# A two-layer decoder trunk in float32: which operand of its large products stands still

## Chip, core and metric

One core of one Trainium2 chip runs the whole program. The metric is the time of one execution in device microseconds (us), as the median of several runs.

## The reference

The reference takes 256 tokens of 2048 features through two layers, all in float32, and returns 256 x 2048 numbers. Cut to what matters:

```python
# layer 0
h = rms_norm(x) * (1 + scale0) + shift0          # scale, shift, gate = silu(c) @ ada_w + ada_b
p = h @ hg_w_in[0]                               # 2048 x 7440
x = x + gate0 * (concat(rwkv7(p), gated_deltanet(p)) @ hg_w_out[0])     # 2048 x 2048
x = x + gate1 * swiglu(rms_norm(x) * (1 + scale1) + shift1)             # 2 x 2048 x 5632, 5632 x 2048
# layer 1
p = modulated_norm(x) @ ssm_w_in[0]              # 2048 x 10304
x = x + gate2 * (mamba2(p) @ ssm_w_out[0])       # 4096 x 2048
x = x + gate3 * swiglu(modulated_norm(x))
return rms_norm(x) * final_norm_w
```

`swiglu(h)` is `(silu(h @ w1) * (h @ w3)) @ w2`. The mixers (RWKV-7, gated DeltaNet, Mamba-2) are recurrences over the tokens, worked in chunks of 128 tokens. The four modulations are products of one row, `silu(c)`, with four matrices of 2048 x 6144.

## The kernel before

**Large products.** Everything is kept with features on the partitions: an activation is 16 row blocks (kt) of 128 features x 256 tokens. A weight matrix is cut into tiles of 128 x 128. A product is made in float32 accuracy from two narrow parts of each operand: `split` (line 743) writes the rounded `hhi` and the rest `hlo`; `split_next` (line 623) rounds the weights to `whi` on the scalar engine (ACT) and `low_parts` (line 657) takes the rest `wlo` on the vector engine (DVE). `products` (line 703) then issues three matmuls for each weight tile: the weight tile is the stationary operand, the 256 tokens move through it.

```python
PE.matmul(ps, w(hi, i), ahi[:, kt, :], start=a, stop=False)
PE.matmul(ps, w(hi, i), alo[:, kt, :], start=False, stop=False)
...
PE.matmul(ps, w(lo, i - lag), ahi[:, kt, :], start=False, stop=z)
```

The sum, 128 features x 256 tokens, takes half a bank of PSUM. `lin_tile` (line 678) makes one such column block over all kt. `lin_slab` (line 729) opens a phase: it takes 7 or 8 column blocks at once, kt by kt, so that it can begin when the norm has made the first row block; `clear` (line 725) first writes zeros into each of its banks, with one matmul of 512 columns.

**Streams.** All weights come in the order of their use, up to 1024 columns x 128 rows (512 KB) at a time, through SyncE's queue (SP) into five raw tiles. The modulation weights come in between as half rows; each is a multiply and reduce on DVE (`ada_half`, line 584), 384 in all.

**Phases.** Layer 0's input projection (`in0`, 59 column blocks, with zeros that fill up one of them), the mixers beside it, the output projection (`out0`, begun while the last heads still run), a SwiGLU (`ffn`, line 824, in two halves of the hidden features), layer 1's input projection (`in1`, 81 column blocks, half of one filled up with zeros) beside the Mamba mixer, its output projection (`out1`, two halves), a second SwiGLU. The results of `out0`, `ffn` and `out1` go tile by tile into `out_tiles` (line 803): DVE adds gate times the sum to `x`, ACT squares, DVE sums the squares for the next norm.

**Order.** The program has one order per engine, made while it is traced. A model of the engines' times (`Clock`, line 233) says when each instruction runs. The mixers are chains of small steps (`spawn`, line 458); `products` looks at them after each weight tile, and `run` (line 444) places a step once the model has it ready 600 ns before TensorE's (PE's) present place. `force` (line 464) places steps, soonest first, until a condition holds, whether or not the engines have to wait for them; `bank` (line 413) calls it where fewer than four banks are free for a new sum. So PE, DVE and ACT run in a fixed order in which the chains' instructions stand between those of the stream.

**What takes a sum from PSUM.** With features on the partitions, the convolution (`conv_silu`, line 1024), the token shift (`shift`, line 1227), the gates (`z_gate`, line 1245, and `gate_part`, line 1678), the SwiGLU product (in `ffn`) and `out_tiles` read the sums directly. Only two narrow blocks are turned to tokens on partitions, by `tok_major` (line 1055).

## Time and profile before

| | |
|---|---|
| median of 3 runs | 3018.11 us (3016.45 to 3021.1) |
| the profiled execution: first to last instruction | 3020.2 us |
| TensorE (PE) busy | 2876.4 us, 95% |
| its weight loads (PEld) busy | 2804.5 us, 93% |
| DVE busy | 2216.3 us, 73% |
| ACT busy | 1436.8 us, 48% |
| read from HBM | 695.70 MB |

A row of the timeline gives start, length, engine and operation of one instruction, or of several alike in succession (x4); a matmul names the bank that it writes, then its moving and its stationary operand. PE's matmuls are pipelined: each is listed with its whole length, though the next starts long before it ends, so the price of one in a stream is the distance from its start to the next one's. A row of the stages gives for a stretch of time the busy time and instruction count of each engine, the clock granted to PE, the DMA share and GB/s. Nearly all instructions carry one source line, L351, that of a helper that records them.

### The profile page before, as it was taken

To read this page: it belongs to the slowest core of one execution; us is meant where nothing else is said; L and a number is where in the kernel's file an instruction comes from. 1 tells how busy PE (TensorE), PEld (TensorE's weight loads), DVE (VectorE), ACT (ScalarE), POOL (GpSimd) and SP (SyncE) were. 2 spreads that over 40 slices of the span, in tenths; PEclk is the share of its full clock that TensorE was granted. 3 is DMA by queue.
4 is the path that set the end of the run, shared out by engine and by line. 5 is a ranking of instruction groups with operands and counts; after the bars stand their busy time and mean duration, and the time that the engine had idled before them with its cause. 6 is when DMAs were issued, how large, how long until landed. Compare 5 with 4: busy or idle time off the path is not lost.

```text
span 3020.2 us, 61379 instructions
## 1 busy us (share of the span) xinstructions
PE 2876.4 (95%) x25033; PEld 2804.5 (93%) x25033; DVE 2216.3 (73%) x3546; ACT 1436.8 (48%) x2353; POOL 115.0 (4%) x159
## 2 busy tenths in 40 slices
PE   3699999998799999999999999999999999999998
PEld 3599898988799999999999999999999999999998
DVE  6988888988677787777767878888867754554555
ACT  2254555545444444444446556555445444444444
POOL 0000001000000000000000111111000000000000
PEclk8799999999999999999999999999999999999999
DMA  7977566667687898877865666666866756656554
GB/s 278 355 250 222 175 201 215 188 223 287 220 283 275 280 334 312 286 269 262 262 207 203 204 215 228 215 232 218 283 223 221 278 189 176 199 184 192 185 173 153
DMA packets 236667, 706.29 MB, mean 234 GB/s; under 512 B 37296, under 2 KB 56032, under 8 KB 236128
## 3 DMA queue, kind: packets, MB, share of 16 engines
q1 hardware_dynamic: 235808, 699.46, 68.9%
q8 instruction: 195, 3.19, 0.4%
q10 hardware_dynamic: 576, 2.92, 0.3%
q14 instruction: 88, 0.72, 0.1%
HBM read 695.70 MB, written 6.58 MB: 233 GB/s over the span
## 4 chain that ended last, share of the span: by engine, by line
issue 51%; PE 21%; DVE 2%; ACT 1%; POOL 0%; DMA 0%; DVEq 0%; POOLq 0%; ACTq 0%
PE bank L351 21%; DVE wlo L351 1%; ACT whi L351 1%; DVE hlo L351 0%; DVE adat L351 0%; DVE t0b L351 0%; DVE x L351 0%; DVE w L351 0%; POOL mgsa L351 0%; DVE ymix L351 0%; DMA adat<-in_ada 0%; DVE mar L351 0%; ACT t L351 0%; DVE mxs L351 0%; ACT hhi L351 0%
## 5 line engine op out<-in xcount | busy, mean ns | idle before, releaser
L351 PE MATMUL bank<-hhi,whi 128*128 128x256 f32 x5568 | 1485.8, 288 | 71.0 <-ACT whi L351 68.8
L351 PE MATMUL bank<-hlo,whi 128*128 128x256 f32 x5568 | 1459.6, 284 | 2.9 <-DVE hlo L351 2.6
L351 DVE TENSOR_TENSOR wlo<-raw,whi 128x1024 fp32r<-128x1024 f32 (+3 forms) x997 | 1111.0, 1128 | 393.8 <-ACT whi L351 389.9
L351 ACT ACTIVATE whi<-raw 128x1024 fp32r<-128x1024 f32 (+3 forms) x997 | 965.2, 977 | 697.5 <-PE bank L351 641.6
L351 PEld LDWEIGHTS bank<-hhi,whi 128*128 128x128 f32 x5568 | 1066.1, 191 | 95.7 <-ACT whi L351 79.3
L351 PE MATMUL bank<-hhi,wlo 128*128 128x256 f32 x5568 | 1131.3, 285 | 6.3 <-DVE wlo L351 5.9
L351 PEld LDWEIGHTS bank<-hlo,whi 128*128 128x128 f32 x5568 | 1067.2, 192 | 6.6 <-DVE hlo L351 4.6
L351 PEld LDWEIGHTS bank<-hhi,wlo 128*128 128x128 f32 x5568 | 864.8, 191 | 15.0 <-DVE wlo L351 9.2
L351 PE MATMUL bank<-ghi,whi 128*128 128x256 f32 x1408 | 351.2, 282 | 0.2 <-ACT whi L351 0.2
L351 PE MATMUL bank<-glo,whi 128*128 128x256 f32 x1408 | 351.2, 282 | 0.0
L351 PEld LDWEIGHTS bank<-ghi,whi 128*128 128x128 f32 x1408 | 265.1, 188 | 0.4 <-ACT whi L351 0.4
L351 PEld LDWEIGHTS bank<-glo,whi 128*128 128x128 f32 x1408 | 265.2, 188 | 0.0
L351 PE MATMUL bank<-ghi,wlo 128*128 128x256 f32 x1408 | 229.7, 282 | 0.0
L351 DVE CUSTOM_DVE_ANT_0 adat<-adat,silc,adap 128x1024 f32<-128x1024 f32 x160 | 211.8, 1323 | 21.4 <-DMA adat<-in_ada 20.6
L351 DVE CUSTOM_DVE_ANT_0 adat<-adat,silc,prm 128x1024 f32<-128x1024 f32 x160 | 208.4, 1303 | 14.2 <-DMA adat<-in_ada 14.1
L351 PEld LDWEIGHTS bank<-ghi,wlo 128*128 128x128 f32 x1408 | 193.9, 188 | 0.0
L351 ACT ACTIVATE fs<-bank 128x256 f32<-128x256 f32 x88 | 33.7, 383 | 189.2 <-PE bank L351 189.2
L351 DVE TENSOR_TENSOR fg<-fs,bank 128x256 f32<-128x256 f32 x88 | 37.0, 421 | 115.2 <-ACT fs L351 115.2
L351 DVE SCALAR_TENSOR_TENSOR w<-pad,prm,w 128x256 f32<-128x256 f32 x216 | 110.1, 511 | 5.1
L351 DVE SCALAR_TENSOR_TENSOR x<-bank,mod,x 128x256 f32<-128x256 f32 x106 | 50.6, 482 | 45.9 <-PE bank L351 45.5
L351 POOL TENSOR_TENSOR rstd<-rpow,half_neg 128x2 f32<-128x2 f32 x5 | 4.4, 890 | 1768.6 <-DVE rpow L351 1768.6
L351 DVE TENSOR_TENSOR glo<-fg,ghi 128x256 fp32r<-128x256 f32 x88 | 37.4, 425 | 42.6 <-ACT ghi L351 42.6
(251 smaller groups left out, 2011.5 us busy)
## 6 DMA issues: line engine op xcount, KB each, us to landing
raw<-in_ffn SPq DMA_DIRECT2D x352, 512.0 KB, 4.4
adat<-in_ada SPq DMA_DIRECT2D x320, 512.0 KB, 4.5
raw<-in_in SPq DMA_DIRECT2D x266, 512.0 KB, 3.8
raw<-in_ffn SPq DMA_DIRECT2D x128, 384.0 KB, 4.5
raw<-in_ffn SPq DMA_DIRECT2D x128, 320.0 KB, 3.0
raw<-in_out SPq DMA_DIRECT2D x75, 512.0 KB, 4.6
raw<-in_ada SPq DMA_DIRECT2D x64, 512.0 KB, 5.3
mar<-sscr SPq DMA_DIRECT2D x16, 512.0 KB, 7.7
```

Source lines behind the costliest of these rows:

```text
L351: r = f(*a, **k)
```

## The change

The large products swap their operands. The stationary operand is now a 128 features x 128 tokens block of the activation, and up to 512 columns of weights move through it. Each row block of weights and column block of width w takes six matmuls: for both halves of the tokens the high and the low part of the activation against `hi`, then the high part against `lo`. The sum has tokens on the partitions and fills two banks (`pair`), one for each half of the tokens. Column blocks are 512 wide in both `ffn`, in `out1`, in the z gates and in half of `out0`; 384 wide (three heads' columns; once 400 and once 448, with the narrow blocks that were filled up with zeros before) in the rest of the projections; 256 wide twice. A piece of weights still holds at most 1024 columns: two units of 384 or 512.

What reads the sums still wants features on the partitions. So a sum is copied from PSUM to SBUF (`evac`, or the first step of a gate or of SwiGLU, or the addition of an earlier part), and `turn` brings each 128 columns of it back with two transposes on TensorE, two blocks into one bank; then the old steps follow. The SwiGLU product is taken with tokens on partitions and turned once. The first half of `ffn` is kept in SBUF with tokens on the partitions, instead of being added to `x`. `clear`, `tok_major` and the zeros are gone. The order of layer 0's heads is another, and the order model has new prices for the stream's matmuls. Comments are dropped too. The core of the diff:

```diff
-ORDER0 = [(q[0], int(q[1:])) for q in "r0 r1 g0 r2 z0 r3 g1 r4 z1 r5 g2 r6 r7 g3 z2 z3".split()]
+ORDER0 = [(q[0], int(q[1:])) for q in "r0 r1 r2 g0 r3 z0 g1 r4 r5 g2 r6 r7 g3 z1".split()]
...
+LAG = 3
...
+def _in0():
+    out, c = [(0, 256)], 256
+    for k, j in ORDER0:
+        for n in {"r": [400 if j == 2 else 384], "g": [384, 384], "z": [512]}[k]:
+            out.append((c, n))
+            c += n
+    return out
+def _in1():
+    out, c = [], 0
+    for g in range(8):
+        for n in (448 if g == 0 else 384, 384, 512):
+            out.append((c, n))
+            c += n
+    return out
+IN0, IN1 = _in0(), _in1()
+SLAB0, SLAB1 = 3, 2
...
+def by_cols(block, kts=range(16), m=0):
+    c, n = block
+    kts, w = list(kts), COLS // n
+    return [[(m, k, c, n) for k in kts[i:i + w]] for i in range(0, len(kts), w)]
...
-    def release(t):
-        busy.discard(next(q for q in range(8) if banks[q] is t))
+    def pair(spare=SPARE):
+        force(lambda: len(busy) <= 6 - spare)
+        return [bank(True, 0) for _ in range(2)]
+    def release(*ts):
+        for t in ts:
+            busy.discard(next(q for q in range(8) if banks[q] is t))
...
-    def lin_tile(ps, act, kts, first=True, last=True):
...
+    def lin(acc, block, act, kts=range(KT), first=True, last=True, need=None):
...
+            products([(acc, k, n, first and k == a, last and k == z) for _, k, _, n in us], hi, lo, act)
+            del kts[:len(us)]
...
+    def slab(accs, act, ahead):
+        for kt in range(KT):
+            for k in range(LEAD + 1 if kt == 0 else 1):
+                k = kt + LEAD if kt else k
+                if k < KT:
+                    ahead(k)
+            hi, lo, us = next_piece()
+            assert [u[1] for u in us] == [kt] * len(accs)
+            products([(acc, kt, u[3], kt == 0, kt == KT - 1) for acc, u in zip(accs, us)], hi, lo, act)
...
+    def products(us, hi, lo, act):
+        n = len(us)
         lag = min(LAG, n)
+        at = [sum(u[2] for u in us[:i]) for i in range(n)]
+        def tick():
+            low_parts()
+            issue_raw()
+            run()
+            if max(clock.at(ET.DVE), clock.at(ET.Activation)) < clock.at(ET.PE) + SOON:
+                prefetch()
+            fill_ada()
         for i in range(n + lag):
             if i < n:
+                acc, k, w, a, z = us[i]
+                for t in range(2):
+                    for e in range(2):
+                        PE.matmul(acc[t][:, :w], act[:, k, e, t * P:(t + 1) * P], hi[:, at[i]:at[i] + w],
+                                  start=a and e == 0, stop=False)
+                    tick()
             if i >= lag:
+                acc, k, w, a, z = us[i - lag]
+                for t in range(2):
+                    PE.matmul(acc[t][:, :w], act[:, k, 0, t * P:(t + 1) * P],
+                              lo[:, at[i - lag]:at[i - lag] + w], start=False, stop=z)
+                tick()
...
-    def clear(b):
-        PE.matmul(b, zeros.to_broadcast([P, P]), zeros.to_broadcast([P, 512]), start=True, stop=False)
...
+    def evac(acc, dst, n):
+        for t in range(2):
+            S.activation(dst[t][:, :n], acc[t][:, :n], AF.Copy)
+        release(*acc)
+    def turn(o, tm, c):
+        for t in range(2):
+            tp(o[:, t * P:(t + 1) * P], tm[t][:, c * P:(c + 1) * P])
...
+    def out_block(l, x, nxt, m, n, tm):
+        for q in range(0, n // P, 2):
+            w = min(2, n // P - q)
+            ps = bank()
+            for i in range(w):
+                turn(half(ps, i), tm, q + i)
+            out_tiles(l, m + q, [half(ps, i) for i in range(w)], x, nxt)
+            yield
+    def out_new(l, x, nxt, m, n, acc, tms):
+        tm, = yield from take(tms, 1)
+        evac(acc, tm, n)
+        yield
+        yield from out_block(l, x, nxt, m, n, tm)
+        tms.append(tm)
+    def out_more(l, x, nxt, m, n, acc, part):
+        for t in range(2):
+            V.tensor_tensor(part[t][:, :n], part[t][:, :n], acc[t][:, :n], ALU.add)
+        release(*acc)
+        yield
+        yield from out_block(l, x, nxt, m, n, part)
...
+            def gated(acc, own):
+                own += yield from take(tms, 1)
+                for i in range(2):
+                    S.activation(own[0][i], acc[i], AF.Silu)
+                release(*acc)
+            def hidden(acc, own, k):
+                tm = own[0]
+                for i in range(2):
+                    V.tensor_tensor(tm[i], tm[i], acc[i], ALU.mult)
+                release(*acc)
+                yield
+                for q in range(0, 4, 2):
+                    ps = bank()
+                    for i in range(2):
+                        turn(half(ps, i), tm, q + i)
+                    hi = g2x[:, k + q:k + q + 2, 0, :]
+                    S.activation(hi, n2(ps), AF.Copy)
+                    V.tensor_tensor(g2x[:, k + q:k + q + 2, 1, :], n2(ps), hi.bitcast(F32), ALU.subtract)
+                    yield
+                tms.append(tm)
...
+                        lin(accs[0], (0, 512), h2)
+                    made.append(spawn(hidden(accs.pop(0), own, 4 * b), after=[c]))
+                for m in range(4):
+                    acc = pair()
+                    lin(acc, (0, 512), Rows(g2x, 4 * first), range(4 * first, 4 * (first + nb)),
+                        need=lambda k: made[k // 4 - first].done)
+                    o = [part[:, i, 512 * m:512 * m + 512] for i in range(2)]
+                    if h == 0:
+                        spawn(keep(acc, o))
                     else:
+                        spawn(out_more(l, x, (l + 1, t), 4 * m, 512, acc, o))
...
-    def conv_silu(ps, items):
...
+    def conv_silu(tm, items, free=None):
...
         pads = yield from take(pfree, len(items))
         ws = yield from claim(len(items))
         tl = []
+        for n, ((o, q, w, bias), c) in enumerate(zip(items, pads)):
+            if n % 2 == 0:
+                ps = bank()
+            src = half(ps, n % 2)
+            turn(src, tm, q)
...
...
+                    ready(a, b, ymix, chain_of)
+                    for i, q in enumerate(OUT_A):
+                        if a == 0:
+                            accA.append(pair())
+                        lin(accA[i], q, h2, range(a, b), a == 0, False)
+                for q, o in zip(OUT_B, pB):
+                    acc = pair(2)
+                    lin(acc, q, h2, range(c))
+                    spawn(keep(acc, o, q[1]))
...
+            with tc.tile_pool(name="yo0", bufs=1, reuse_waits="tile") as fp:
+                tms = tm_tiles(fp, 3, "o")
+                ready(c, KT, ymix, chain_of)
+                for a, b, o in zip(OUT_A, OUT_B, pB):
+                    acc = accA.pop(0)
+                    lin(acc, a, h2, range(c, KT), False, True)
+                    spawn(out_new(0, x, (1, t), a[0] // P, a[1], acc, tms))
+                    acc = pair(2)
+                    lin(acc, b, h2, range(c, KT))
+                    spawn(out_more(0, x, (1, t), b[0] // P, b[1], acc, o))
+                for q in OUT_C:
+                    acc = pair()
+                    lin(acc, q, h2)
+                    spawn(out_new(0, x, (1, t), q[0] // P, q[1], acc, tms))
+                drain()
...
-    def shift(items):
...
+    def shift(tm, items):
         pads = yield from take(pfree, len(items))
+        for n, ((o, q, muc, omu), c) in enumerate(zip(items, pads)):
+            if n % 2 == 0:
+                ps = bank()
+            src = half(ps, n % 2)
+            turn(src, tm, q)
+            S.activation(c[:, 3:], src, AF.Copy, scale=prc("mu", muc))
+            S.activation(o, src, AF.Copy, scale=omu[:, muc:muc + 1])
+        yield
+        for (o, q, muc, omu), c in zip(items, pads):
+            V.tensor_tensor(o, o, c[:, 2:2 + T], ALU.add)
         pfree.extend(pads)
...
+        z = [ws.get() for _ in range(2)]
+        for t in range(2):
+            S.activation(z[t], acc[t][:, o:o + T], AF.Tanh, scale=0.5)
+        yield
+        for t in range(2):
+            V.scalar_tensor_tensor(z[t], z[t], 1.0, acc[t][:, o:o + T], ALU.add, ALU.mult)
+        own.append(j)
+        if len(own) == 3:
+            release(*acc)
+        yield
+        ps = bank()
         for i in range(2):
+            turn(half(ps, i), z, i)
         for i in range(2):
             h = 2 * j + i
             y = ymix[:, 8 + h, :]
             if h in g0["done"]:
+                V.tensor_tensor(y, y, half(ps, i), ALU.mult)
             else:
+                S.activation(y, half(ps, i), AF.Copy)
                 g0["gate"].add(h)
...
+        def gate(acc, g):
+            z, = yield from take(tms, 1)
+            for t in range(2):
+                S.activation(z[t], acc[t], AF.Tanh, scale=0.5)
+            yield
+            for t in range(2):
+                V.scalar_tensor_tensor(z[t], z[t], 1.0, acc[t], ALU.add, ALU.mult)
+            release(*acc)
+            yield
+            for q in range(0, 4, 2):
+                ps = bank()
                 for i in range(2):
+                    turn(half(ps, i), z, q + i)
+                S.activation(ymix[:, 4 * g + q:4 * g + q + 2, :], n2(ps), AF.Copy)
...
+        def conv_part(acc, items, n, dt=False):
+            tm, = yield from take(tms, 1)
+            if dt:
+                for i in range(2):
+                    S.activation(raw[:, 64 * i:64 * i + 64], acc[i][:, 384:448], AF.Copy)
+            evac(acc, tm, n)
+            yield
+            yield from conv_silu(tm, items, lambda: tms.append(tm))
```

More of the change, by code (lines that the diff above doesn't have):

```diff
@@ new lines, in _in0, with units @@
+def _in0():
[14 more added lines that the diff above has]
+SLAB0, SLAB1 = 3, 2
+def units(phase):
+    if phase in ("in0", "in1"):
+        b, n = (IN0, SLAB0) if phase == "in0" else (IN1, SLAB1)
+        return by_rows(b[:n]) + sum((by_cols(q) for q in b[n:]), [])
@@ L146, in _stream @@
-def _stream(blocks, phase):
-    out = []
-    for b in blocks:
-        o = 0
-        for n in halves(b.shape[1]):
-            out.append(b[:, o:o + n])
-            o += n
-    assert [b.shape[1] for b in out] == sizes(phase)
-    return np.concatenate([b.reshape(-1) for b in out])
+        r = []
+        for a, b in zip(CUTS, CUTS[1:-1]):
+            for q in OUT_A:
+                r += by_cols(q, range(a, b))
+        for q in OUT_B:
+            r += by_cols(q, range(c))
+        for q in zip(OUT_A, OUT_B):
+            for z in q:
+                r += by_cols(z, range(c, 16))
@@ L158, in _percol, with width, _stream @@
+    return r
+def width(piece):
+    return sum(u[3] for u in piece)
+def _stream(phase, *mats):
+    return np.concatenate([
+        np.concatenate([mats[m][k * P:(k + 1) * P, c:c + n] for m, k, c, n in piece], 1).reshape(-1)
+        for piece in units(phase)])
 def _percol(v):
@@ L191, in prepare @@
     w = i["hg_w_in"][0]
-    order = [w[:, 7424:7440], np.zeros((2048, P - 16), np.float32), w[:, 3072:3328]]
+    order = [w[:, 3072:3328]]
     for k, j in ORDER0:
@@ L1037, in conv_silu @@
             tl.append((o, w, c, y))
-        release(ps)
+        if free is not None:
+            free()
         yield
@@ L1121, in half, with ready @@
         return b[:, i * T:(i + 1) * T]
-    def both(ps, kts, first, last):
-        if len(kts) <= 4:
-            lin_tiles([half(ps, i) for i in range(2)], h2, kts, [first] * 2, last)
-        else:
-            for i in range(2):
-                lin_tile(half(ps, i), h2, kts, first, last[i])
-    def partial(a, b, ymix, chain_of, pss):
+    def ready(a, b, ymix, chain_of):
         force(lambda: all(c.done for q in YORDER0[a:b] for c in chain_of[q]))
@@ L1206, in mixer0 @@
                 for i in range(2):
[L1207 to L1214 removed]
+                    cv.append(spawn(gdn_head(sums(), own, i, 2 * j + i), after=cv[1:]))
@@ L1630, in layer1 @@
     def layer1(x, told):
-        pss = [bank(True, 2) for q in range(4)]
-        lin_slab([pss[0][:, 0:T]] + [p[:, i * T:(i + 1) * T] for p in pss[1:] for i in range(2)], h2,
-                 norm_mod(2, told))
+        accs = [pair(2) for q in range(SLAB1)]
+        slab(accs, h2, norm_mod(2, told))
         close_x(told)
@@ L1717, in mixer1, with sums @@
         ssd, ends, zs = [], [], []
+        blocks = list(IN1)
+        def sums():
+            q = blocks.pop(0)
+            if accs:
+                return accs.pop(0)
+            acc = pair()
+            lin(acc, q, h2)
+            return acc
         for g in range(8):
```

505 lines of the change are left out of this document (191 added, 314 removed).

## The prediction

> **What bounds the kernel now.** I read the page of the profile first (busy shares), then the stages, then the groups of instructions on TensorE, then the timeline around single matmuls.
>
> ```profile
> span 3020.2 us, 61379 instructions
> ...
> PE 2876.4 (95%) x25033; PEld 2804.5 (93%) x25033; DVE 2216.3 (73%) x3546; ACT 1436.8 (48%) x2353; POOL 115.0 (4%) x159
> ```
>
> ```profile
> core 0: us, PE busy (x) PEld busy (x) DVE busy (x) ACT busy (x) POOL busy (x), PEclk, DMA share, GB/s
> 36.00:150.00 114.00, 67.38 (x338) 62.89 (x336) 106.21 (x182) 28.88 (x46) 0.25 (x5) 0.75 0.96 352
> 150.00:765.00 615.00, 585.93 (x5989) 542.15 (x5990) 527.10 (x1172) 324.69 (x720) 41.81 (x89) 0.98 0.67 221
> 765.00:1530.00 765.00, 753.58 (x6324) 750.91 (x6324) 565.12 (x779) 334.87 (x439) 0.00 (x0) 1.00 0.81 279
> 1580.00:2060.00 480.00, 476.70 (x4091) 464.15 (x4090) 400.36 (x615) 287.52 (x522) 56.07 (x42) 1.00 0.65 221
> 2300.00:3005.00 705.00, 705.00 (x5983) 704.82 (x5982) 389.00 (x466) 313.50 (x408) 0.00 (x0) 1.00 0.62 198
> ```
>
> The five stretches are the start, layer 0's mixers with `out0`, the first SwiGLU, `in1` with its mixer, and the second SwiGLU. From 150 us on PE is the engine that is never free: the last stretch has no gap at all, at the full clock. It holds little but the stream's matmuls, so 705.00 us / 5983 = 118 ns is the price of one matmul with 256 columns. The start is different: there DVE (106 of 114 us) and the DMA (0.96) are full and PE is not. In layer 0 DVE follows closely, 527 of 615 us.
>
> ```profile
> L351 PE MATMUL bank<-hhi,whi 128*128 128x256 f32 x5568 | 1485.8, 288 | 71.0 <-ACT whi L351 68.8 <-ACT hhi L351 1.2
> ...
> L351 PE MATMUL bank<-ghi,whi 128*128 128x256 f32 x1408 | 351.2, 282 | 0.2 <-ACT whi L351 0.2
> ...
> L351 PE MATMUL bank<-yhi,whi 128*128 128x256 f32 x256 | 66.6, 282 | 0.0
> ...
> L351 PE MATMUL bank<-cst,mxs 128*128 128x128 f32 x64 | 9.6, 272 | 0.0
> ```
>
> The first three counts give 7232 weight tiles (5568 + 1408 + 256), each with three matmuls: 21696 x 118 ns = 2560 us of the 3020 are the stream. The fourth row is a transpose, used below.
>
> **Why 118 ns, and what 512 columns cost.** The kernel has a few matmuls with 512 columns in the midst of the stream, the clears.
>
> ```profile
> 638.65 0.38 PE L351 MATMUL bank<-zeros 128*128 128x512 f32 x1
> 638.65 0.19 PEld L351 LDWEIGHTS bank<-hhi,whi 128*128 128x128 f32 x1
> 638.87 0.28 PE L351 MATMUL bank<-hhi,whi 128*128 128x256 f32 x1
> 638.87 0.19 PEld L351 LDWEIGHTS bank<-hlo,whi 128*128 128x128 f32 x1
> 638.99 0.28 PE L351 MATMUL bank<-hlo,whi 128*128 128x256 f32 x1
> ...
> 656.26 0.38 PE L351 MATMUL bank<-zeros 128*128 128x512 f32 x1
> ...
> 656.47 0.28 PE L351 MATMUL bank<-hhi,whi 128*128 128x256 f32 x1
> ```
>
> Each load of a stationary operand starts together with the matmul before its own; so one load is under way at a time, and with 256 columns the matmul follows its load by 0.12 us. With 512 columns the next matmul follows after 0.22 and 0.21 us, though twice 118 is 236. That is what one sees if the columns pass at 0.42 ns each (215 / 512; 256 of them would take 108) and a load takes about 118, whichever is longer. I take 215 ns for 512 columns, 161 for 384, 168 for 400, 188 for 448, and 118 for 256, where the load still sets the pace. The clears move one broadcast zero, not data; real data of 512 columns, in plain float32, stands here:
>
> ```profile
> 1655.01 1.02 PE L351 MATMUL bank<-mxw,mbtok 128*128 128x512 f32 x2
> 1655.47 0.69 PE L351 MATMUL bank<-hhi,whi 128*128 128x256 f32 x1
> 1655.99 0.28 PE L351 MATMUL bank<-hlo,whi 128*128 128x256 f32 x1
> ```
>
> From 1655.01 to 1655.99 lie two records of the float32 product and one stream matmul: (0.98 - 0.118) / 2 = 0.43 us a record, twice the clear's 0.215 as if the columns passed twice, at the same 0.42 ns. The Trainium skill ("TensorE: Matmul & The Clock Gate", Back-to-back issue gap) gives N / 2.4 + 2.5 ns, 216 ns for 512 columns, and by it the new stream is some 10 us dearer than by my row. For 256 columns it gives 109: by that rule alone the old stream would take 2369 us, the change would save 33 instead of the 233 below, and the time would be 3094. The 118 of this trace contradicts it, so this gets no chance of its own.
>
> **The new stream.** Six matmuls for each row block and column block. 512 columns: both first halves of SwiGLU 2 x 22 x 96, the second halves 2 x 44 x 4 x 6, `out1` 768, gates 10 x 96, `out0` 2 x 96, together 8256 x 0.215 = 1775 us. 384: 32 blocks x 96 = 3072 x 0.161 = 495. 256: 192 x 0.118 = 23. 400 and 448: 96 x (0.168 + 0.188) = 34. Sum 2327 us against 2560: 233 us less, 8 of them from the dropped zeros (176 columns) and the rest from the wider matmuls.
>
> **The transposes.** Column tiles that are turned: 58 in `in0`, 16 in `out0`, 44 + 16 in each SwiGLU, 80 in `in1`, 32 in `out1`: 306, with two transposes each, 612.
>
> ```profile
> 1738.98 0.60 PE L351 MATMUL bank<-cst,mxs 128*128 128x128 f32 x4
> 1739.34 0.37 PE L351 MATMUL bank<-hhi,whi 128*128 128x256 f32 x1
> 1739.54 0.28 PE L351 MATMUL bank<-hlo,whi 128*128 128x256 f32 x1
> ```
>
> From 1738.98 to 1739.54 lie four transposes and one stream matmul: (0.56 - 0.118) / 4 = 0.11 us each, with nothing lost at the change of kind. 612 x 0.11 = 67 us, all on PE and so all on the path. The Trainium skill (same page, PE-mode transpose) speaks against this: about 275 ns in a kernel. The trace disagrees inside a stream.
>
> **What of the gain doesn't reach the end.** At the head of each phase the slab isn't PE's:
>
> ```profile
> 1536.00:1573.00 37.00, 36.11 (x279) 34.03 (x278) 24.39 (x41) 17.86 (x28) 0.00 (x0) 0.98 0.50 151
> 2257.00:2302.00 45.00, 45.00 (x360) 43.65 (x359) 30.05 (x46) 22.52 (x32) 0.00 (x0) 0.99 0.43 142
> 765.00:815.00 50.00, 43.29 (x332) 41.04 (x332) 35.86 (x57) 20.59 (x30) 0.00 (x0) 0.99 0.62 202
> ```
>
> One matmul takes 133, 125 and 151 ns there; the norm's steps and the splits set the pace. I count no gain for the SwiGLU slabs (2 x 16 x 24 x 118 ns = 45.3 each before, 192 x 215 ns = 41.3 after: 4 + 4 lost), half of it for `in1` (3 lost) and none for the first slab (3 lost): 14 us back.
>
> **The ends of the phases.** They get longer:
>
> ```profile
> 3006.23 0.75 PE L351 MATMUL bank<-ghi,wlo 128*128 128x256 f32 x5
> 3007.02 0.48 DVE L351 SCALAR_TENSOR_TENSOR x<-bank,mod,x 128x256 f32<-128x256 f32 x1 [3.89 <-PE bank L351]
> 3007.54 0.42 ACT L351 ACTIVATE sq<-x 128x256 f32<-128x256 f32 x1 [5.50 <-DVE x L351]
> 3007.98 0.42 DVE L351 TENSOR_TENSOR sqacc<-sqacc,sq 128x256 f32<-128x256 f32 x1 [0.48 <-ACT sq L351]
> 3008.46 0.66 PE L351 MATMUL bank<-cst,sqacc 128*128 128x64 f32 x4 [1.48 <-DVE sqacc L351]
> ```
>
> ```profile
> L351 DVE TENSOR_TENSOR mxdt<-bank,s1hdt 128x512 f32<-128x512 f32 x16 | 11.0, 686 | 4.7 <-PE bank L351 4.6
> ```
>
> Now one tile is left after the last matmul: 1.44 us to the norm's sum. Then it is four: two additions of 512 columns from PSUM (1.37), four transposes (0.44), two updates of x (0.96), two sums (0.84), two more updates (0.96), a square and a sum (0.84), and some 0.5 between engines: 5.9, so 4.5 us more at the ends of both SwiGLUs and of `out1`. `out0` ends with two tiles (2 us more), and between the halves of `out1` the program now drains four (2.5): 18 us.
>
> **The mixers.** ACT gets the copies out of PSUM; it has 290 of 615 and 192 of 480 us free and the 50 to 60 copies in either take at most 0.69 us each (DVE's price for 512 columns, above), 41 us, so they cost nothing as work. As a wait they stand between a sum and its transposes: on PE the stream's matmuls queue behind a transpose whose copy is late. `run` places it only when the order model has it ready 0.6 us before, so I count little, except where `pair` forces steps because four banks are taken. DVE's work hardly changes, and the stage gets shorter: its slack in layer 0 falls from 88 to about 63 us, and if PE's unbusy 29 us grow in that ratio, 11 are added; in `in1` 1. I take 12 (bounds 0 and 44, below). SwiGLU's DVE goes from 565 / 765 to about 565 / 715, still covered. The clears that go lie mostly where PE waits anyway: 2 us. Weight bytes, modulation rows and SP's order of them stay.
>
> **Sum.** 3020.2 - 233 + 67 + 14 + 18 + 12 - 2 = 2896 for the profiled execution, which lies 2 us over the median of the runs: 2894 us.
>
> **Rivals.** (1) *DVE and the chains become the bound in the mixers.* For it: 86% DVE in layer 0, and chains that are longer by a copy and two transposes. Against it: PE is busy there now. The net gain of these stages is 37 - 16 in layer 0 and 41 - 18 in `in1`, 44 us; if they last as long as now, 2894 + 44 - 12 = 2926, and with the 34 us of transposes on top 2960. (2) *The 118 ns are a price of columns, 0.461 ns each*, because rounded data can't pass faster and a clear's zero can. Then the 5.54 million columns of the new stream cost 2553 us, nothing is won, the slabs lose nothing, and transposes, ends and waits stay: 2894 + 226 - 14 = 3106, slower. It decides from 227 ns for 512 columns on: there the saving of 109 us just pays for the rest. Against it speak the two clears and the float32 product. (3) *A transpose costs its whole length*, 272 ns in its group's row, because pairs of them come alone behind a copy: 612 x 0.163 = 99 more, 2994. Against it: the four in a row above. This is also what the Trainium skill's 275 ns would make of it.
>
> **Chances.** Forecast 0.73, (1) 0.16, (2) 0.07, (3) 0.04; of (2) 0.01 lies near its threshold, where nothing changes. Were the slabs and mixers free and the ends half as dear, the time would be 2859, which is why the low end is 2845, with a few us for the 0.01 us in which the clears are read (0.21 instead of 0.215 is 41 us less, but the float32 row, 0.43, speaks for 0.215). The high end, 2955, takes in most of (1). A measurement of this kernel can tell about 0.2% from no change; faster 0.93 (forecast, (1) and (3)), same 0.01, slower 0.06.
>
> **What the new profile would show.** Stream matmuls with 512 columns starting 0.21 to 0.22 us apart and PEld busy about half of the time; the second SwiGLU between slab and end near 655 us instead of 705; transposes 0.11 us apart in their groups; 5 to 7 us without a matmul before each norm's sum; DVE about 90% in layer 0. The forecast is wrong in its core if 512 columns take 0.227 us or more; it is too low if PE waits for ACT's copies or for DVE in layer 0 by tens of us.

## The result and the profile after

The changed kernel takes 3119.35 us (median of 4, 3115.71 to 3121.46) against 3017.94 us (4 runs, 3016.45 to 3021.1): ratio 1.0329, 95% interval 1.0315 to 1.0344. It is slower by 101 us where 124 us less were forecast. The profiled execution took 3119.03 us.

The page after, spans and busy times:

```profile
span 3117.2 us, 42297 instructions
...
PE 2901.8 (93%) x15636; PEld 2422.7 (78%) x15636; DVE 2189.4 (70%) x3396; ACT 1475.7 (47%) x2374; POOL 103.8 (3%) x159
```

PE has 9397 instructions less and is still busy 25 us longer; and its weight loads are busy for 78% of the time, where half was expected. The stages of the changed kernel, in the columns of the prediction's second fence (start, layer 0 with `out0`, first SwiGLU, a part of `in1`, second SwiGLU behind its slab):

```profile
36.00:150.00 114.00, 64.94 (x252) 59.51 (x252) 105.55 (x181) 29.33 (x46) 0.20 (x4) 0.76 0.97 353
150.00:765.00 615.00, 565.12 (x4676) 483.81 (x4676) 498.43 (x1142) 328.18 (x765) 37.77 (x88) 0.96 0.64 206
765.00:1530.00 765.00, 746.93 (x3326) 606.73 (x3326) 551.39 (x693) 329.99 (x385) 0.70 (x1) 0.99 0.79 275
1640.00:2130.00 490.00, 461.68 (x2652) 410.24 (x2651) 372.85 (x583) 288.40 (x534) 49.79 (x42) 0.99 0.60 198
2390.00:3100.00 710.00, 706.07 (x3113) 574.09 (x3112) 365.75 (x356) 298.25 (x326) 0.00 (x0) 1.00 0.56 191
```

Two things stand here. The second SwiGLU has PE busy almost all the time (706.07 of 710.00 us) at the full clock, and it has not become shorter: the 705 us of before were to become 655. And in the mixers' stages PE is busy for 565 of 615 us (586 before) and for 462 of 490: there it waits, though DVE has become less busy (498 for 527 us). The price of a product is read from two places of PE's timeline:

```profile
900.37 1.99 PE L362 MATMUL bank<-whi,h 128*128 128x512 f32 x8
902.20 1.08 PE L362 MATMUL bank<-wlo,h 128*128 128x512 f32 x4
...
1104.18 2.03 PE L362 MATMUL bank<-whi,g2x 128*128 128x512 f32 x8
1106.04 1.10 PE L362 MATMUL bank<-wlo,g2x 128*128 128x512 f32 x4
```

Eight products lie between 900.37 and 902.20, (1.83 / 8 =) 229 ns each, and between 1104.18 and 1106.04, 233 each; over all pairs without a wait in the trace the mean is 230, and 173 for 384 columns. And the waits of PE:

```profile
PE bank L362 <- ACT whi L362: 73.7, 41, 8.7
PE bank L362 <- DVE sqacc L362: 41.9, 5, 28.9
PE bank L362 <- ACT w L362: 29.9, 24, 2.9
PE bank L362 <- ACT Big L362: 10.9, 8, 2.9
PE bank L362 <- DVE wlo L362: 8.7, 13, 1.9
```

The first two are mostly the start, which was there before (68.8 us for `whi`). The waits for ACT's `w` and `Big` are new: 41 us in 32 waits. What they are, one step of `conv_silu` shows:

```profile
1640.96 0.38 PE L362 MATMUL bank<-cst,tmm 128*128 128x128 f32 x2
1641.38 0.38 ACT L362 ACTIVATE pad<-bank 128x256 f32<-128x256 f32 x1 [1.54 <-PE bank L362]
1641.66 0.56 ACT L362 ACTIVATE w<-bank,prm 128x256 f32<-128x256 f32 x1
1642.27 0.42 PEld L362 LDWEIGHTS bank<-cst,tmm 128*128 128x128 f32 x4 [1.17 <-ACT w L362]
1642.27 0.66 PE L362 MATMUL bank<-cst,tmm 128*128 128x128 f32 x4 [0.93 <-ACT w L362]
```

A block is turned with two transposes into the first half of a bank, ACT reads it twice, and only then, 0.93 us later, PE turns the next block into the other half of the same bank. The whole stream stands behind that transpose.

Where the 101 us are is best read between the norms: each norm starts with four products of `sqacc` on PE, and the starts of the first of them cut the program into four stages. In us, with the kernels of the experiments; the stages are from one profiled execution of each kernel, the last column is the median of its runs:

| | layer 0, `out0` | first SwiGLU | layer 1 | second SwiGLU | median |
|---|---|---|---|---|---|
| before | 728.8 | 773.5 | 720.9 | 755.2 | 3018 |
| after | 782.0 | 767.7 | 764.7 | 761.8 | 3119 |
| e2_turnfirst | 756.3 | 772.2 | 761.2 | 762.5 | 3098 |
| e3_turnfirst_price | 748.0 | 802.9 | 739.4 | 770.6 | 3103 |
| e5_price_mixers | 753.3 | 771.5 | 739.8 | 762.7 | 3070 |
| e6_turn_twice | 783.4 | 779.0 | 790.7 | 774.5 | 3174 |
| e7_ffn_wide | 731.4 | 763.7 | 741.4 | 749.0 | 3031 |
| e9_ffn_wide_fill | 733.4 | 763.0 | 721.1 | 749.0 | 3008 |

The SwiGLUs, where 50 us each were to be won, came out at -6 and +7; the mixers' stages lost 53 and 44.

### The profile page after: what moved, and what is told of

It is laid out like the page before. It is cut to its first block, busy times and chain, and to the rows that moved or that the text cites. A ratio compares the mean times of both kernels' runs of the same rounds, so it can differ in the third digit from the quotient of the medians.

```text
span 3117.2 us, 42297 instructions
## 1 busy us (share of the span) xinstructions
PE 2901.8 (93%) x15636; PEld 2422.7 (78%) x15636; DVE 2189.4 (70%) x3396; ACT 1475.7 (47%) x2374; POOL 103.8 (3%) x159
## 5 line engine op out<-in xcount | busy, mean ns | idle before, releaser
L362 PE MATMUL bank<-whi,h 128*128 128x512 f32 (+3 forms) x6144 | 1478.4, 380 | 79.3 <-ACT whi L362 73.7
L362 PEld LDWEIGHTS bank<-whi,h 128*128 128x128 f32 x6144 | 1132.0, 192 | 270.8 <-ACT whi L362 94.6
L362 PE MATMUL bank<-wlo,h 128*128 128x512 f32 (+3 forms) x3072 | 798.5, 380 | 8.8 <-DVE wlo L362 8.7
L362 PEld LDWEIGHTS bank<-wlo,h 128*128 128x128 f32 x3072 | 566.4, 193 | 98.2 <-DVE wlo L362 15.9
L362 PE MATMUL bank<-whi,g2x 128*128 128x512 f32 x1408 | 356.9, 395 | 0.0
L362 PEld LDWEIGHTS bank<-whi,g2x 128*128 128x128 f32 x1408 | 264.5, 188 | 62.1
L362 PE MATMUL bank<-wlo,g2x 128*128 128x512 f32 x704 | 195.2, 396 | 0.0
L362 PEld LDWEIGHTS bank<-wlo,g2x 128*128 128x128 f32 x704 | 131.5, 188 | 30.0
L362 PE MATMUL bank<-whi,y 128*128 128x512 f32 x256 | 65.0, 395 | 1.2 <-ACT y L362 0.6
L362 PEld LDWEIGHTS bank<-whi,y 128*128 128x128 f32 x256 | 48.1, 188 | 12.8 <-DVE y L362 0.9
L362 PE MATMUL bank<-cst,tmm 128*128 128x128 f32 x192 | 31.1, 278 | 21.2 <-ACT w L362 20.5
```

The source lines that it names most:

```text
L362: r = f(*a, **k)
```

## Experiments

My theory after the result: the saving is missing because a product of 512 columns costs 230 ns and not 215, and the mixers lose time in waits that the sum had at 12 us. Its rivals: for the price, a cause that lies in this kernel (accumulation, data, the other engines) and could be taken away; for the mixers, that they are bound by the added transposes or by DVE.

### The price by itself

```diff
+        for i in range(N):
+            t, e = i // 2 % 2, i % 2
+            lhs = st[s][:, 2 * t + e, :]
...
+            rhs = mv[s][:, :w]
...
+            PE.matmul(b[t][:, :w], lhs, rhs, start=one or i in (0, 2), stop=one or i in (N - 3, N - 1))
```

Each stretch has 64 products (N), tiles of its own and one thing changed.

> This kernel computes nothing of the reference: it holds only 15 stretches of 64 matmuls each, with stationary and moving operands as in the changed kernel, and passes x through to the output. The changed kernel's stream took 229 to 232 ns for 512 columns, where the clears and the plain float32 product gave 214 to 215. Each stretch changes one thing. (a) Traffic theory: the other engines and the DMA disturb PE's reads; then the plain stretches (first, idle, again) take 214 ns and those with DVE, ACT or DMA beside them (vect, scal, load) 229. (b) Accumulation theory: adding to PSUM costs; then the stretch in which every matmul starts a new sum (new) takes 214, all others 229. (c) Moving-read theory: distinct columns in the rounded type pass more slowly than one broadcast column; then broad takes 214 and new, stat, same and zero 229. (d) Load theory: the load of a stationary operand costs the matmul beside it about 15 ns; then stat (one stationary column, broadcast) takes 214 and the rest 229. (e) Data theory: zeros pass faster; then the stretch with a moving operand of zeros (zero) takes 214. By rival (2) of the prediction, a price by column alone, 384, 256 and 128 columns take 0.45 ns a column, 173, 115 and 58; if a load sets the floor, 256 and 128 columns both take about 118.

In the timeline a stretch is one row; from its start to the next one's start, over 64, is the price (the x192 row is 384, 256 and 128 columns together):

```profile
27.86 14.67 PE L31 MATMUL bank<-mvfirst,stfirst 128*128 128x512 f32 x64
42.37 14.67 PE L31 MATMUL bank<-mvnew,stnew 128*128 128x512 f32 x64
56.88 14.15 PE L31 MATMUL bank<-mvbroad,stbroad 128*128 128x512 f32 x64
70.87 14.67 PE L31 MATMUL bank<-mvzero,stzero 128*128 128x512 f32 x64
...
114.69 26.05 PE L31 MATMUL bank<-mvc,stc 128*128 128x384 f32 x192
```

(42.37 - 27.86) / 64 = 226.7 ns, the same with a new sum each time (new), with zeros as data, with one stationary tile all the time, and beside ScalarE or loads; beside VectorE it is 228.1 over the stretch and 227 by the median of its records. Only the broadcast moving operand is cheaper: (70.87 - 56.88) / 64 = 218.6. A broadcast stationary operand costs 231. By single records 384 columns take 173.7, 256 take 119.8, 128 take 111. The three widths above 128 lie on one line, 13.4 ns + 0.4167 ns a column; 13.4 ns is the time of 32 columns. So the price belongs to the product itself, and none of the causes that were taken away brings 214. The line also says what the 118 ns of the kernel before were: 13.4 + 106.7 = 120 for 256 columns. They were set by columns and a fixed part. A floor, which I take for that of the load, shows only near 111, with 128 columns.

### Both blocks turned before either is read

```diff
             if n % 2 == 0:
                 ps = bank()
+                for i, it in enumerate(items[n:n + 2]):
+                    turn(half(ps, i), tm, it[1])
             src = half(ps, n % 2)
-            turn(src, tm, q)
```

in `conv_silu` and in `shift` of the changed kernel.

> The changed kernel, but the convolution and the token shift first turn both blocks of a bank and then read them. Theory: in the changed kernel the two transposes of a bank's second block wait on PE until ACT has read the first block twice (0.93 us and more, once in each of 33 steps, 42 us in all in its list of PE's gaps); without that the kernel is 35 to 45 us faster than the changed kernel: 3075 to 3085 us, ratio to the kernel before 1.019 to 1.022. Rival: the chains are late anyway (DVE and ACT in the mixers), so that the wait only moves to the next step: less than 15 us gained, ratio over 1.028.

Measured: 3097.8 us, ratio to before 1.0255 (1.024 to 1.0271), so 21.5 us less than the changed kernel: neither the 35 to 45 nor the under 15. PE's waits:

```profile
PE bank L362 <- ACT whi L362: 79.8, 44, 8.8
PE bank L362 <- DVE sqacc L362: 43.0, 5, 29.6
PE bank L362 <- DVE wlo L362: 16.5, 16, 2.1
```

The rows for ACT's `w` and `Big` are gone, all 41 us of them. Layer 0 takes 26 us less. In layer 1, where 20.5 us of them stood, 10 come back as waits for the weights' two parts (`whi` from 5.8 to 11.6 us, `wlo` from 1.8 to 6.0 in that stage) and 4.5 as waits for POOL's `mgr` and `mgsa`; only 4 us are won. The wait is real and was half covered by the next one.

### The order model with the measured price

```diff
-                return max(118.0, 0.418 * nn)
+                return max(118.0, 7.0 + 0.434 * nn)
```

on top of e2_turnfirst.

> The same with a new price in the order model alone: 7 + 0.434 ns per column, as the changed kernel's matmuls measured, in place of 0.418 ns per column. Theory: the order model thinks PE 7% faster than it is, so splits and chain steps are placed later in PE's order than the chip would like; with the measured price the remaining waits shrink a little: 3065 to 3080 us. Rival: the waits come from what the chains need, not from the model's price: within 5 us of the kernel without the new price.

Measured: 3102.83 us, ratio 1.0273 (1.0253 to 1.0293), no gain. But the stages part: layer 0 -8 us, layer 1 -22, the first SwiGLU +31 (PE waits 17 us there for DVE's `tmf`, 18 times), the second +8. So the same price was given to the mixers alone:

```diff
-                return max(118.0, 0.418 * nn)
+                return max(118.0, 0.418 * nn + (7.0 + 0.016 * nn) * Clock.measured)
...
     def ffn(l, x, told, tnew):
+        Clock.measured = 0.0
...
+        Clock.measured = 1.0
```

> The changed kernel with both blocks of a bank turned before ScalarE reads either (3097.8 us), and with the measured price of a product in the order's model, but only outside the SwiGLUs, where the old price stays. Theory (the model's price too low lets the mixers' chain steps come too early, and in the SwiGLUs the same low price happens to load the vector engines less): layer 0's stage near 748 us instead of 756, layer 1's near 740 instead of 761, the SwiGLUs near 770 and 762 as without it, 3065 to 3075 us in all. Rival (the 21 us that layer 1 won with the price everywhere came from the weights that were ready after a slower SwiGLU): layer 1 stays near 761 and the whole within 8 us of 3098.

Measured: 3069.91 us, ratio 1.0163 (1.0147 to 1.0178): inside the expected 3065 to 3075, with layer 1 at 739.8 and both SwiGLUs as without it. (Layer 0, at 753.3 for 748, gave less.) `run` places a chain's step when the model says that it is ready; with products of 384 columns priced 13 ns too low, the model's PE is early and, as I read it, DVE's and ACT's steps stand elsewhere than the engines' real times would have them. The truer price is worth 28 us here. The order model of the kernel before was as far off (0.425 x 256 = 109 ns for products that take 118), and that kernel was not run with the true price: how much of the 28 us came with the change is not shown. Why the truer price harms the SwiGLUs was not settled.

### Every turn twice

```diff
     def turn(o, tm, c):
-        for t in range(2):
-            tp(o[:, t * P:(t + 1) * P], tm[t][:, c * P:(c + 1) * P])
+        for _ in range(2):
+            for t in range(2):
+                tp(o[:, t * P:(t + 1) * P], tm[t][:, c * P:(c + 1) * P])
```

> The changed kernel with every turn of a block back to features on partitions issued twice, into the same place: 612 transposes more, nothing else. Theory (they stand in the stream at 0.11 us each, as the sum had them): 67 us slower than the changed kernel, 3186 us, ratio 1.056. Rival 1 (most of them stand where TensorE waits for ScalarE anyway): 20 to 45 us slower, 3140 to 3165. Rival 2 (a transpose costs 0.27 us with its turn-around): 165 us slower, 3284.

Measured: 3173.61 us, ratio 1.0511 (1.0494 to 1.0527), 54 us over the changed kernel: 54 / 612 = 0.089 us for each added transpose. The theory had 67 us, rival 1 20 to 45. The stages say why: +1 in layer 0, +11, +26 and +13. In layer 0 they hide in waits; elsewhere they are on the path at about their price in a stream. Rival 2 falls. An added transpose stands right behind its twin, so this run alone can't show what a change of kind costs; the changed kernel's own trace does: where four transposes stand between products of 512 columns and nothing waits (49 times), they add 0.11 us each to the products' 230 ns, the change back included. With that the third rival of the prediction falls too.

### What the fixed part belongs to

```diff
+        k = {"s64": 64, "s32": 32}.get(s, P)
...
+            lhs = st[s][:, 2 * t + e, :k]
+            rhs = mv[s][:, :w]
+            if s == "both":
+                lhs = st[s][:, 0, 0:1].to_broadcast([P, P])
+            if s in ("both", "b256") or s == "alt" and i % 2:
+                rhs = mv[s][:, 0:1].to_broadcast([P, w])
```

> Does none of the reference's work: stretches of 64 products of 512 columns on constant data, each stretch with its own tiles and one thing changed, so only the start-to-start time inside a stretch is read. Known from the first such kernel: 226.7 ns for 512 columns, 173.7 for 384, 119.8 for 256, 218.7 when the moving operand is one column broadcast, and 0.215 for the clears of the kernel before, whose two operands are both broadcast. That is 13.4 ns + 0.4167 ns a column. Theory A (the 13.4 ns belong to the load of the stationary tile, whose reads take time from the moving tile's): they shrink with the number of stationary columns, so 220 ns with 64 stationary columns and 217 with 32; both operands broadcast gives 214-215 as in the clears. Theory B (a fixed price for each product, whatever is loaded): 227 with 64 and with 32 stationary columns; a broadcast moving operand is cheaper for a reason of its own, and both broadcast gives 219. Both: 320 moving columns take 146.7 by the line, every other product with a broadcast moving operand 222.7, 256 broadcast columns 112-116, all into one bank 226.7, plain float32 430. In one stretch VectorE, ScalarE and DMA work at once beside it: 226.7 if the 230 ns of the changed kernel come from something else, 229-232 if from the three together.

```profile
41.54 14.15 PE L31 MATMUL bank<-mvboth,stboth 128*128 128x512 f32 x64
55.53 14.60 PE L31 MATMUL bank<-mvalt,stalt 128*128 128x512 f32 x64
69.97 29.71 PE L31 MATMUL bank<-mvs,sts 128*64 128x512 f32 x128
99.51 7.33 PE L31 MATMUL bank<-mvb,stb 128*128 128x256 f32 x64
...
128.02 55.09 PE L31 MATMUL bank<-raw,x 128*128 128x512 f32 x128
182.55 15.10 PE L31 MATMUL bank<-mvonebank,stonebank 128*128 128x512 f32 x64
```

Both operands broadcast take (55.53 - 41.54) / 64 = 218.6 ns. The stretches with 64 and 32 stationary columns take (99.51 - 69.97) / 128 = 231: not less, rather more, so theory A falls. B's 227 is the nearer, though 4 ns too low. 256 broadcast columns take 112, a record of plain float32 with 512 columns 429 (each of those 64 products has two records) and 320 columns 147, both by the median of single records, the three engines together 226.7.

The fixed part depends on the clock. From 110.07 to 120.31 us the granted clock is 0.50, and the products of 320 columns that fall into it follow one another after 266 or 267 ns, twice the 133.3 of their columns and nothing more. So the 13.4 ns are not a number of TensorE's cycles that every product costs; what they are stays open.

The stretch "alt" shows what misled the prediction. In its records the distance after a broadcast product is 215 ns, and after the normal one beside it 232 to 239; the pair takes as long as two normal products ((69.97 - 55.53) / 64 = 225.6). So a broadcast product among others can read as 215 without being worth it. Around the two clears that the prediction read (214 each in the records) no neighbour pays so much, though: the products before and after them take 116 and 120, and 114 and 119 ns, in a stream of 118.

### From 227 to 230

> Does none of the reference's work: stretches of 64 products on constant data, each behind one product with a mark of its own. Open is why 512 columns take 226.7 ns by themselves and 230 to 233 in the changed kernel (and 256 columns 119.8 by themselves and 117.7 in the kernel before), though VectorE, ScalarE and DMA beside them change nothing. Theory A (what changes from product to product decides, where each operand lies): 226.7 in the first stretch (four stationary tiles in turn, one moving tile), and 229 to 233 where the moving tile, the stationary tile or both change as in the kernel; 117 to 118 for 256 columns in the order of the kernel before. Theory B (something of the whole program, such as the waits between the engines): 226.7 in every stretch of 512, 119.8 in every one of 256.

```diff
+            if s in ("four2", "n4"):
...
+                rhs = hi[i % 4][:, 0:w]
...
+            if s == "turn":
...
+                lhs = act(k, e, t)
+            if s == "lag":
...
+                lhs, rhs = act(k, e, t), hi[k // 2 % 4][:, k % 2 * w:k % 2 * w + w]
```

"four2" has another moving tile every product, "turn" another stationary one, "lag" both as in the changed kernel. By the median of single records every stretch of 512 columns has 227 ns and every one of 256 has 120, also in the order of operands of the two kernels: theory A falls. Then for 0.145 ms at a time, and with the engines' work for the whole of it:

```diff
+        n = 160 if s in ("warm", "again") else 640
...
+                for z in range(int(us / 2.0)):
+                    SP.dma_start(into[z % 4], I["w"][:, z % 4])
...
+                for _ in range(int(us / 1.25)):
+                    V.tensor_tensor(lo, raw, hi.bitcast(F32), ALU.subtract)
...
+                for _ in range(int(us / 1.05)):
+                    S.activation(h3, raw, AF.Copy)
```

> Does none of the reference's work: stretches of 640 products (0.145 ms for 512 columns) on constant data, alone, beside VectorE, beside ScalarE, beside loads from DRAM, and beside all three for the whole of the stretch (the earlier stretches were 64 products, with six loads at most). Still open is the step from the 226.7 ns of every short stretch to the 230 to 233 in the changed kernel, 30 to 50 us over its 8256 products of 512. Theory A (load on the chip over longer than 15 us slows the products): 229 to 233 in the last such stretch of 512, 226.7 in the one alone, and the one that makes the difference shows it alone. Theory B (the program itself, with its waits and signals between engines): 226.7 in all of them, and 119.8 in both of 256.

```profile
49.12 145.31 PE L31 MATMUL bank<-hi,st 128*128 128x512 f32 x640
...
629.94 145.31 PE L31 MATMUL bank<-hi,st 128*128 128x512 f32 x640
...
852.06 77.00 PE L31 MATMUL bank<-hi,st 128*128 128x256 f32 x640
```

The stretch alone and the one beside everything take the same 145.31 us: theory A falls here too. What makes 230 of 227 (some 28 us in 8256 products) and 118 of 120 in the kernel before stays open. B, the program's waits and signals, is what is left, and the changed kernel's trace speaks against it: where no wait stands between them, products of 512 columns that send a signal are followed by the next after 230.0 ns (1269 of them), the others after 230.2 (6619). From 2500 to 2518 us the distances run 226, 229, 232 over and over, through products with a signal and without.

### Wide products where no transposes are needed

The price says what is left to win: 227 to 230 ns for 512 columns against 2 x 118. That can be had without swapping the operands, in the kernel before: in the SwiGLUs, but for their slabs, the high part of a weight tile stays stationary and the high and the low part of the activations, side by side, move through it at once.

```diff
-                PE.matmul(ps, w(hi, i), ahi[:, kt, :], start=a, stop=False)
-                PE.matmul(ps, w(hi, i), alo[:, kt, :], start=False, stop=False)
+                PE.matmul(ps[0], w(hi, i), ahi.t[:, kt], start=a, stop=False)   # [high | low], a whole bank
...
+                            b = bank(True)
+                            lin_tile((b,), h2, range(KT))
+                            S.activation(v[q], b[:, T:2 * T], AF.Copy)
+                            V.tensor_tensor(v[q], b[:, 0:T], v[q], ALU.add)
...
+                    V.scalar_tensor_tensor(x[:, m, :], ps[:, T:2 * T], modc(l, 2, m), x[:, m, :], ALU.mult, ALU.add)
```

> The kernel before, with weights stationary as it was, and in the SwiGLUs alone (but for the first eight column blocks) 512 moving columns: the high and the low part of the activations lie side by side, the high part of a weight tile meets both in one product into a whole bank, the low part meets the high one in a product of 256; the two halves of the bank are added on VectorE behind a ScalarE copy. 3968 weight tiles take 230 + 118 = 348 ns instead of 3 x 118 = 354, or 227 + 118 = 345: 24 to 37 us less by the price that the first experiment found, less 2 to 5 us for longer ends of the phases: 2985 to 2998 us, ratio 0.989 to 0.993. Rival (a 512-column product costs the same as two of 256 once loads are counted, and the added work on VectorE holds up the chains' copies): 3018 or more, ratio 1.000 to 1.005.

Measured: 3031.3 us, ratio 1.0035 (1.0022 to 1.0048), inside the rival's range. Its first reason doesn't hold: the SwiGLUs won 9.8 and 6.2 us. In these stages a product of 512 columns takes 232 ns in the records and one of 256 takes 118.5, 351 together, so 1984 x (354 - 351) = 6 us each come from the products. Its second, that work added on VectorE holds something up, does, but not in the SwiGLUs: layer 1, whose products are untouched, lost 20.5. Its waits on PE and its modulation rows on DVE:

```profile
PE bank L351 <- ACT whi L351: 13.1, 10, 3.2
PE bank L351 <- DVE sqacc L351: 4.4, 1, 4.4
PE bank L351 <- DVE wlo L351: 4.3, 3, 2.5
```

```profile
L351 DVE CUSTOM_DVE_ANT_0 adat<-adat,silc,prm 128x1024 f32<-128x1024 f32 x37 | 51.0, 1379 | 0.9 <-DMA adat<-in_ada 0.9
L351 DVE CUSTOM_DVE_ANT_0 adat<-adat,silc,adap 128x1024 f32<-128x1024 f32 x38 | 50.1, 1320 | 1.5 <-DMA adat<-in_ada 1.3
```

75 half rows of modulations are worked there, 61 before: the SwiGLU's DVE, now with one more operation for each column block, had left 14 to the next layer (`fill_ada` takes one only when the model has DVE 0.5 us behind PE). One figure answers this:

```diff
-                until = clock.at(ET.PE) + (LATE if due <= st["item"] else FILL)
+                until = clock.at(ET.PE) + (LATE if due <= st["item"] else st["fill"])   # 0.0 in the SwiGLUs
```

> The kernel of 3031 us (the one before, with 512 moving columns in the SwiGLUs alone), which won 9.8 us in the first SwiGLU and 6.2 in the second and lost 20.5 in layer 1. Changed is one figure of the order: in the SwiGLUs a half row of modulations may be taken as soon as the model has VectorE free, not only when it is 0.5 us behind. Theory (the 14 half rows that the busier VectorE left to layer 1, 75 there for 61, hold up the weights there): layer 1 is back at 721 to 726 us, the SwiGLUs stay within 2 us of 764 and 749, 3008 to 3014 us in all, ratio 0.996 to 0.998. Rival (layer 1 lost its time to the other layout of the activations, or because the weights are no longer far ahead at the end of a faster SwiGLU): layer 1 stays over 735, ratio 1.002 or more.

```profile
PE bank L352 <- POOL mgsa L352: 2.5, 1, 2.5
PE bank L352 <- DVE sqacc L352: 2.0, 1, 2.0
...
PE bank L352 <- DVE wlo L352: 1.4, 3, 0.8
```

```profile
L352 DVE CUSTOM_DVE_ANT_0 adat<-adat,silc,adap 128x1024 f32<-128x1024 f32 x31 | 46.7, 1507 | 0.7 <-DMA adat<-in_ada 0.7
L352 DVE CUSTOM_DVE_ANT_0 adat<-adat,silc,prm 128x1024 f32<-128x1024 f32 x31 | 43.6, 1405 | 0.7 <-DMA adat<-in_ada 0.7
```

Measured: 3008.14 us, ratio 0.9954 (0.9939 to 0.9969). 62 half rows, no wait for `whi` left in layer 1, 721.1 us there: the theory holds, and this version is a little faster than both kernels, 13 us under the kernel before, which took 3020.98 us beside it.

## Why the prediction was wrong

It missed by 225 us (2894 against 3119), and on the wrong side.

**The step that failed is the price of 512 columns**, "I take 215 ns for 512 columns, 161 for 384". It measured 230 and 173: 8256 x 0.015 + 3072 x 0.012 = 161 us, and 3 more for 400 and 448. The new stream costs 8256 x 0.230 + 3072 x 0.173 + 59 = 2489 us, so it saves some 70 us of 2560, not 233. The step rested on two readings, and both were right as readings, but neither is the price of these products:
- The clears' 0.22 and 0.21 us. Their operands are broadcast: with a broadcast moving operand the runs have 218.6 in e1_price and e4_fixed, and 215 where every other product has one, though the pair there is hardly cheaper than two normal ones. The prediction named that reservation ("one broadcast zero, not data") and went on.
- Float32's 0.43 us a record, twice 215. It measured 429 in e4_fixed. But it stands for another kind of product, without the fixed part (429 = 2 x 213.3 + 2), so it was no second witness for the rounded one.

What followed was a law, "whichever is longer" of a load of 118 ns and 0.42 ns a column, by which 256 columns were bound by the load. The line of e1_price says 13.4 ns + 0.4167 ns a column: 256 columns were bound by the same thing as 512, and doubling the width saves one fixed part of 13.4 ns, not 21; in the kernels themselves it saved 2 x 118 - 230 = 6. The Trainium skill ("TensorE: Matmul & The Clock Gate", Back-to-back issue gap) has, for the gap of a single matmul, the same slope with a fixed part of 2.5 ns, 216 ns for 512 columns. The 226.7 of e1_price contradicts it by 11, and its agreement with the clear was no proof of either.

**The second rival** had the sign and the point from which it decides, 227 ns. The measured 230 lies just past it. Its mechanism, 0.461 ns for each column, is not what happened (512 columns would take 236), and that its 3106 comes near 3119 is chance: its products are too dear, and the waits below are missing in it.

**The mixers' waits** were taken as 12 us within 0 and 44. Two things were not seen. The prediction looked for PE's waits at the copies ahead of the transposes; they stand between the two turns of one bank: 41 us, of which e2_turnfirst won 21.5 back. The Trainium skill ("PSUM — Partial Sum Buffer", PSUM bank collisions) says that accesses of different engines are to be kept apart by bank, not by address. The trace shows what such a guard costs here, 0.93 us of PE waiting for ACT's signal before it writes a half bank that ACT does not read; no run leaves the guard out. Second, the order model got the same too low price as my sum; the truer one is worth 28 us (e5_price_mixers against e2_turnfirst), with the reservation made there. The first rival's cause, DVE as the bound, did not come: DVE went down to 498 of 615 us.

**What held.** Transposes: 67 us in the sum, 54 by doubling them, though each record is 278 to 282 ns long. Ends of the phases, forecast 4.5 us longer at each SwiGLU; the second:

```profile
3097.68 1.09 PE L362 MATMUL bank<-wlo,g2x 128*128 128x512 f32 x4
3099.32 0.33 PE L362 MATMUL bank<-cst,tpart 128*128 128x128 f32 x1 [0.55 <-DVE tpart L362]
3099.92 0.98 PE L362 MATMUL bank<-cst,tpart 128*128 128x128 f32 x7 [0.27 <-DVE tpart L362]
3105.07 1.11 PE L362 MATMUL bank<-cst,sqacc 128*128 128x64 f32 x4 [4.17 <-DVE sqacc L362]
```

From the last product's end at 3098.77 to the sum at 3105.07 are 6.3 us, 1.48 before: 4.8 more. At the first it is 4.1 more, at `out1` 3.8; `out0`'s end did not get longer, where 2 us were counted. The SwiGLU slabs did not win, as said, and lost a little:

```profile
2380.18 2.11 PE L362 MATMUL bank<-whi,h 128*128 128x512 f32 x8
...
2383.26 2.11 PE L362 MATMUL bank<-whi,h 128*128 128x512 f32 x8
```

Twelve products in 3.08 us are 257 ns each, 49 us for the 192, where 45.3 were counted.

**The miss put together:** 164 (price) + 21.5 (turned and read in one bank) + 28 (the model's price) = 214 of 225 us. But the sum held 12 us for the waits already, and its transposes were 13 us too dear, so 214 - 12 - 13 = 189 us are accounted for. For the other 36, some 4 of them the second SwiGLU's slab, no experiment was made. The price alone, 164 us, is more than the 124 us that were to be won and turns them into a loss.

## What to carry to other kernels

A price read from an odd instruction in a stream (a clear, another data type, a broadcast operand) is a price of that instruction; when the whole forecast hangs on it, its threshold is to be compared with the error of the reading, and here 215 stood only 12 ns from the 227 where the sign turns. Wider products save only the fixed part of each, so look first for operands that can be put side by side as they are; a change of layout that adds a transpose for every sum must be paid from that. When a block is turned or written in parts for another engine, write all parts of a bank before the first read, and when a change moves a product's price, the order model's price needs a measurement too.

## What the runs showed of the chip

- A rounded float32 product with its own stationary tile, in a test of its own at the full clock, takes the time of its moving columns plus that of 32 more (226.7, 173.7, 147, 119.8 ns for 512, 384, 320, 256), whatever the data, the sums, the banks or the other engines do. With 64 or 32 stationary columns 512 take 230 to 232. With 128 moving columns it takes 111. At half the clock 320 columns take 267, without the fixed part. In the kernels 512 columns take 230 and 256 take 118. Plain float32 with 512 columns takes 429 a record, and has two records a product.
- A broadcast moving operand saves 8 ns when all products have one (218.6), and 1 ns when every other one has (225.6).
- In a stretch of products with 64 moving columns, back to back with 111 ns each, the granted clock fell to half, although the records show PE busy; then they took 213. In e1_price as many products with 128 columns kept their 111 ns, and what lowered the clock is not shown. In e4_fixed, in the columns of the stages above without those that stand empty there, the stretch of 64 columns begins at 106.68:

```profile
99.51:106.68 7.17, 7.17 (x66) 7.17 (x64) 0.00 (x0) 0.00 (x0) 0.00 (x0) 1.00 0.00 0
...
112.00:117.10 5.10, 5.10 (x26) 5.10 (x26) 0.00 (x0) 0.00 (x0) 0.00 (x0) 0.50 0.00 0
...
121.00:128.00 7.00, 7.00 (x49) 7.00 (x49) 0.00 (x0) 0.00 (x0) 0.00 (x0) 1.00 0.00 0
```

The clock is at 1.00, at 0.50 in the second half of that stretch, and at 1.00 again with 320 columns.
